# The down projection of a decoder block: accumulator loads and stores placed by step, second sums from copies, pools placed anew

## The chip, the cores and the metric

The kernel runs on one core of a Trainium2 chip. The metric is device time in microseconds (us) of one execution; the number for a kernel is the median of its runs. Engines are named as in the profile: PE is TensorE's matmuls, PEld its weight loads, DVE VectorE, ACT ScalarE, POOL GpSimd, SP the engine on whose queue this kernel issues its DMAs.

## The reference

One layer of a decoder: three token mixers side by side, an output projection, then a SwiGLU feed-forward block with its residual. All of it is float32. The change is in the last line, the down projection, the last stage of the kernel.

```python
D_MODEL = 1024; SEQ = 2048; D_FF = 2816
...
    x = x + mixed @ w_out[li]
    hn = rms_norm(x, norm_ffn_g[li])
    gate, up = jnp.split(hn @ w_ffn_up[li], 2, axis=-1)
    x = x + (jax.nn.silu(gate) * up) @ w_ffn_down[li]
return x
```

## The kernel before

A float32 matmul is done as three: each operand is split into a high part that the array takes exactly and the rest, and high x high, high x low and low x high are summed in PSUM. ACT makes the high part (L249, a copy that rounds), and VectorE or POOL the low part (L250, a difference).

The two feed-forward matmuls use a scheme of seven block products in place of eight (Winograd's form of Strassen's). In the **down stage** (L1492 on) the left operand is the gated activation (2048 x 2816), the right one the down weight (2816 x 1024), each cut into two by two blocks. The products are done in the order 1, 5, 6, 2, 3, 7, 4. A product has 11 steps of 128 rows of its inner dimension; each step is 24 matmuls, three for each of the eight PSUM banks (tile `dn`, bank i holds 128 rows by 512 columns of the product). All seven make 1848 matmuls.

For a step SP loads `ar` (left, 512 KB, L1514) and `br` (right, 256 KB, L1503). Products 5 and 7 load two right blocks and take their difference on POOL (L243); 5 keeps it in `xb`, and 6 and 4 go on from there. ACT then writes `dah` and `dbh`, VectorE `dal`, POOL `dbl`. `ar`, `dah`, `dal`, `dbh` and `dbl` have four buffers each, `br` five.

The result is summed in 16 accumulators `acc` of 128 x 1024 (512 KB each), which start as the residual (`x2_s` in DRAM, L1590). Accumulator i (0 to 7) holds the quarters c11 and c12, accumulator 8 + i holds c21 and c22. Behind each product `flush_dn` adds its eight banks to the quarters: product 1 to c11, and ACT keeps a copy `u`; 5 to c12 and c22; 6 to `u`, and `u` then to c21 on VectorE and to c12 and c22 on POOL; 2 to c11, 3 to c12, 7 to c21 and c22, 4 to c21. A half that is finished goes out by a DMA of 256 KB (`done`, L1551): c11 behind product 2, c12 behind 3, c22 behind 7, c21 behind 4.

The order of each engine's instructions is made by a scheduler from the order of the program, the data that each instruction needs and its own estimate of times; what `keep_in_program_order` wraps stays in the order of the program on its queue. An engine takes its instructions in order, and so does SP its DMAs: one that has to wait holds up those behind it. Places in SBUF come from pools; a pool opened at the left grows from low addresses, one at the right from high ones, and a tile placed where an older one lay waits for that one's last use.

Ahead of the down stage lies the **up stage**. For its last block of columns it does the seven products in the same order; its left operands `ah` and `al` of each product have a place of their own. The last product is 4. Behind it DVE and ACT finish the gated block `h` (DVE L1432 reads `c` for the last time), store it (`hs_s`, L1448) and make sums of it for the left operands of products 7, 5, 6 and 3 (`ls`, stored to `ls_s`, L1461).

Of the kernel before, what the change touches and what calls it, by code (L numbers as in the profile page):

```python
# [8 lines left out]
F32 = mybir.dt.float32  # L9
# [4 lines left out]
AF = mybir.ActivationFunctionType  # L14
# [5 lines left out]
P = 128  # L20
T = 2048
D = 1024
NT = T // P
# [39 lines left out]
def hybrid_block(ctx: ExitStack, tc: tile.TileContext, x, norm_mix_g, w_in, gla_w_decay,  # L63
                 gla_b_decay, gla_out_g, sb_q_g, sb_k_g, sb_out_g, hg_out_g, hg_lb_logits,
                 w_out, norm_ffn_g, w_ffn_up, w_ffn_down, out, dbg=None):
    nc = tc.nc
    x, out = x[0], out[0]
    w_in, w_out, w_up, w_dn = w_in[0], w_out[0], w_ffn_up[0], w_ffn_down[0]
    act, dve, pool, pe, dma = nc.scalar, nc.vector, nc.gpsimd, nc.tensor, nc.sync
# [54 lines left out]
    def open_pool(stack, name, bufs, space=None, side=None):  # L124
        kw = {} if space is None else {"space": space}
        if side is not None:
            kw["side"] = side
        return stack.enter_context(tc.tile_pool(name=name, bufs=bufs, reuse_waits="tile", **kw))
# [82 lines left out]
    def dt(name, shape, dtype=F32):  # L211
        return dram.tile(shape, dtype, name=name)
# [14 lines left out]
    x2_s = [dt(f"x2_s{t}", [P, D]) for t in range(NT)]  # L227
# [17 lines left out]
    def add(o, a, b, eng=dve):  # L245
        eng.tensor_tensor(o, a, b, op=ALU.add)  # L246
# [526 lines left out]
    with ExitStack() as ph:  # L773
        cn.open(ph)
        with ExitStack() as p1:
            stg = open_pool(p1, "s_g", 1)
            st = Stage(1, stg, open_pool(p1, "s_x", 2), True)
# [151 lines left out]
    with ExitStack() as ph:  # L929
# [28 lines left out]
        for g in G_ORDER:  # L958
            for h in range(0, SH, 2):
                for c in range(g, -1, -1):  # L960
                    for j in range(2):
                        u = Unit()
# [338 lines left out]

        folds = []
        done, total = 0.0, SH * sum(g + 0.625 for g in range(NG))
        step, wo_step = rec_steps(), load_wo()
        ns, n_slot = 0, 4 * len(units)
# [9 lines left out]
        for n in range(n_slot + LAG_A):  # L1315
            d = 0.0
            if n < n_slot:
                z_step(units[n // 4], n % 4)
                d = (n % 4 + 1) / 16 if units[n // 4].diag else 0.25
# [150 lines left out]
    for ip in range(2):  # L1470
        for n in range(NFF):
            f = n if ip == 0 else n // 2 + NK * (n % 2)
# [17 lines left out]


    pd = ExitStack()  # L1492
    bop = open_pool(pd, "g_bo", 4, side="right")
    lop = open_pool(pd, "g_lo", 4, side="right")
    accp = open_pool(pd, "g_acc", 1)
    rop = open_pool(pd, "g_ro", 1)
    psd = open_pool(pd, "g_psd", 8, PSUM)
    acc = []
# [6 lines left out]
    def left_dn(m, k):  # L1505
        nm = f"{m}_{k}"

        src = lop.tile([P, D], F32, tag="ar", name=f"ar{nm}")
        if m in (1, 2, 4):
            kh, j = {1: (0, 0), 2: (1, 0), 4: (1, 1)}[m]  # L1510
            at = hs_s[kh * NK + k][j].rearrange("p i j t -> p (i j t)")
        else:
            at = ls_s[m][k]
        tc.keep_in_program_order(dma.dma_start(src, at))  # L1514
        hi, lo = (lop.tile([P, D], F32R, tag=x, name=f"{x}{nm}") for x in ("dah", "dal"))
        conv_w(hi, lo, src, dve)
        return hi, lo

    def right_dn(m, k):
        nm = f"{m}_{k}"  # L1520

        def raw(kh, j):
            t_ = bop.tile([P, 512], F32, tag="br", name=f"br{nm}_{kh}{j}", bufs=5)
            load_b(t_, k, kh, j)
            return t_

        if m in (1, 2, 3):
            src = raw(*{1: (0, 0), 2: (1, 0), 3: (1, 1)}[m])
        elif m == 5:
            src = chain_b[k] = rop.tile([P, 512], F32, name=f"xb{k}")  # L1530
            load_b(src, k, 0, 1)
            sub(src, src, raw(0, 0), pool)
        elif m == 6:
            src = chain_b[k]
            sub(src, raw(1, 1), src, pool)
        elif m == 4:
            src = chain_b[k]
            sub(src, raw(1, 0), src, pool)
        else:
            src = raw(1, 1)  # L1540
            sub(src, src, raw(0, 1), pool)
        hi, lo = (bop.tile([P, 512], F32R, tag=x, name=f"{x}{nm}")
                  for x in ("dbh", "dbl"))
        conv_w(hi, lo, src)
        return hi, lo

    held, later = {}, []

    def done(t, hf):
        cs = slice(hf * 512, hf * 512 + 512)  # L1550
        dma.dma_start(out[t * P:(t + 1) * P, cs], acc[t][:, cs])  # L1551

    def flush_dn(m, i, ps):

        c11, c12 = acc[i][:, :512], acc[i][:, 512:]
        c21, c22 = acc[8 + i][:, :512], acc[8 + i][:, 512:]
        if m == 1:
            u = held[i] = rop.tile([P, 512], F32, name=f"u{i}")
            act.activation(u, ps, AF.Copy)
            add(c11, c11, ps)  # L1560
        elif m in (5, 7):
            c = {5: c12, 7: c21}[m]
            add(c, c, ps)
            add(c22, c22, ps)
            if m == 7:
                done(8 + i, 1)
        elif m == 6:
            u = held[i]
            add(u, u, ps)
            add(c21, c21, u)  # L1570
            later.append(lambda: add(c12, c12, u, pool))
            later.append(lambda: add(c22, c22, u, pool))
        else:
            c = {2: c11, 3: c12, 4: c21}[m]
            add(c, c, ps)
            done(*{2: (i, 0), 3: (i, 1), 4: (8 + i, 0)}[m])

    for m in (1, 5, 6, 2, 3, 7, 4):
        pss = [psd.tile([P, 512], F32, tag="dn", name=f"dn{m}_{i}") for i in range(8)]
        for k in range(NK):  # L1580
            (ah, al), (bh, bl) = left_dn(m, k), right_dn(m, k)
            for i in range(8):
                ts_ = slice(i * P, (i + 1) * P)
                pe.matmul(pss[i], ah[:, ts_], bh, start=(k == 0), stop=False)  # L1584
                pe.matmul(pss[i], ah[:, ts_], bl, start=False, stop=False)  # L1585
                pe.matmul(pss[i], al[:, ts_], bh, start=False, stop=(k == NK - 1))  # L1586
            if m == 1 and k == 2:
                for t in range(NT):
                    a = accp.tile([P, D], F32, name=f"acc{t}")
                    tc.keep_in_program_order(dma.dma_start(a, x2_s[t]))  # L1590
                    acc.append(a)
            for fn in later[:2]:
                fn()
            del later[:2]
        for i in range(8):
            flush_dn(m, i, pss[i])
    for fn in later:
        fn()
    pd.close()

    if dbg is not None:
# [29 lines left out]
```

## Time and profile before

| | us |
|---|---|
| median of 3 runs (lowest, highest) | 3063.36 (3062.43, 3068.29) |
| the profiled execution | 3067.76 |
| its span, first to last instruction | 3066.1 |
| last matmul of the up stage to last matmul of the down stage | 2578.05 to 3061.95 |
| PE busy in the whole span | 2796.4 (91%) |
| DVE, ACT, POOL busy in the whole span | 2052.4, 1320.5, 1463.2 |

The times are of one execution. PE's busy time counts pipelined matmuls with ends that are modelled, so a share of 91% says little of a single stage; one reads the stage by its own window and by what PE waited for. A wait is put down to the instruction that came last, and this one may itself have waited; the chain of waits goes further back. The granted clock is the share of full speed that TensorE got; it has two levels, 0.50 (1.2 GHz) and 1.00 (2.4 GHz), and a stretch may hold both.

### The profile page before, as it was taken

To read this page: it belongs to the slowest core of one execution; us is meant where nothing else is said; L and a number is where in the kernel's file an instruction comes from. 1 tells how busy PE (TensorE), PEld (TensorE's weight loads), DVE (VectorE), ACT (ScalarE), POOL (GpSimd) and SP (SyncE) were. 2 spreads that over 40 slices of the span, in tenths; PEclk is the share of its full clock that TensorE was granted. 3 is DMA by queue.
4 is the path that set the end of the run, shared out by engine and by line. 5 is a ranking of instruction groups with operands and counts; after the bars stand their busy time and mean duration, and the time that the engine had idled before them with its cause. 6 is when DMAs were issued, how large, how long until landed. Compare 5 with 4: busy or idle time off the path is not lost.

```text
span 3066.1 us, 45677 instructions
## 1 busy us (share of the span) xinstructions
PE 2796.4 (91%) x15906; PEld 2251.7 (73%) x15906; DVE 2052.4 (67%) x3621; ACT 1320.5 (43%) x2540; POOL 1463.2 (48%) x1412
## 2 busy tenths in 40 slices
PE   5898999998988999988878799999999998899988
PEld 4897778997656666655566588888788887787766
DVE  8887574987767787888877565556777775334233
ACT  5455444445666666765422333333433332322222
POOL 5341454343776666733221344444555553556244
PEclk7999999999788999999989899999999999999999
DMA  3543543343843333234354422222544445742354
GB/s 112 152 125 111 152 129 110 96 136 104 206 144 103 113 115 104 75 113 126 98 192 148 174 90 83 83 83 83 192 151 151 153 154 209 253 148 83 144 190 154
DMA packets 355206, 409.34 MB, mean 134 GB/s; under 512 B 59936, under 2 KB 262944, under 8 KB 353184
## 3 DMA queue, kind: packets, MB, share of 16 engines
q1 hardware_dynamic: 350880, 401.17, 41.1%
q0 software_dynamic: 4096, 5.25, 0.5%
q8 instruction: 127, 2.08, 0.3%
q14 instruction: 103, 0.84, 0.1%
HBM read 281.02 MB, written 125.30 MB: 133 GB/s over the span
## 4 chain that ended last, share of the span: by engine, by line
PE 59%; DVE 12%; DMA 5%; issue 4%; POOL 3%; ACT 2%; SPq 1%; DVEq 0%; POOLq 0%; ACTq 0%
PE gu L1420 9%; PE gu L1421 9%; PE gu L1419 9%; PE dn L1584 4%; PE dn L1585 4%; PE dn L1586 4%; PE z L104 3%; PE av L104 2%; DVE pr L1002 2%; PE wt L107 2%; DVE m L841 1%; PE sch L104 1%; DMA m<-mx_s 1%; PE scg L104 1%; PE ho L104 1%
## 5 line engine op out<-in xcount | busy, mean ns | idle before, releaser
L1420 PE MATMUL gu<-al,uh 128*128 128x512 f32 x1232 | 482.8, 392 | 7.7 <-DVE al L250 7.6
L1419 PE MATMUL gu<-ah,uh 128*128 128x512 f32 x1232 | 481.3, 391 | 4.8 <-ACT ah L249 4.8
L1421 PE MATMUL gu<-ah,ul 128*128 128x512 f32 x1232 | 481.1, 390 | 0.0
L250 POOL TENSOR_TENSOR ul<-bs,uh 128x512 fp32r<-128x512 f32 x176 | 247.7, 1408 | 224.4 <-ACT uh L249 224.4
L1009 POOL TENSOR_TENSOR w<-w,pr 128x512 f32<-128x512 f32 (+1 forms) x174 | 204.1, 1173 | 210.8 <-DVE pr L1002 109.0
L250 POOL TENSOR_TENSOR ul<-us,uh 128x512 fp32r<-128x512 f32 x132 | 186.1, 1411 | 215.5 <-ACT uh L249 185.9
L1584 PE MATMUL dn<-dbh,dah 128*128 128x512 f32 x616 | 238.7, 407 | 46.4 <-ACT dbh L249 46.4
L1420 PEld LDWEIGHTS gu<-al,uh 128*128 128x128 f32 x1232 | 232.2, 188 | 62.2 <-DVE al L250 14.4
L250 DVE TENSOR_TENSOR dal<-ar,dah 128x1024 fp32r<-128x1024 f32 x77 | 114.8, 1495 | 240.4 <-ACT dah L249 231.8
L1419 PEld LDWEIGHTS gu<-ah,uh 128*128 128x128 f32 x1232 | 232.5, 189 | 55.2 <-ACT ah L249 6.5
L1421 PEld LDWEIGHTS gu<-ah,ul 128*128 128x128 f32 x1232 | 232.3, 189 | 47.4
L1585 PE MATMUL dn<-dbl,dah 128*128 128x512 f32 x616 | 241.6, 392 | 4.0 <-POOL dbl L250 4.0
L249 ACT ACTIVATE uh<-bs 128x512 fp32r<-128x512 f32 x176 | 111.0, 632 | 308.0 <-PE gu L1420 284.4
L1586 PE MATMUL dn<-dbh,dal 128*128 128x512 f32 x616 | 240.6, 391 | 1.1 <-DVE dal L250 1.1
L249 ACT ACTIVATE dah<-ar 128x1024 fp32r<-128x1024 f32 x77 | 81.5, 1059 | 315.0 <-PE dn L1585 199.7
L246 DVE TENSOR_TENSOR h<-h,gu 128x512 f32<-128x512 f32 x176 | 120.4, 684 | 144.4 <-PE gu L1421 106.0
L104 PE MATMUL z<-sk,sq 128*128 128x512 f32 (+1 forms) x480 | 169.4, 437 | 14.1 <-ACT w L1001 8.6
L998 ACT ACTIVATE kp<-z 128x512 f32<-128x512 f32 (+1 forms) x240 | 127.8, 532 | 119.3 <-PE z L104 107.6
L1584 PEld LDWEIGHTS dn<-dbh,dah 128*128 128x128 f32 x616 | 120.7, 197 | 73.9 <-ACT dbh L249 48.5
L107 PE MATMUL wt<-ident,w 128*128 128x128 f32 x816 | 148.3, 296 | 14.1 <-POOL w L1009 12.1
L104 PEld LDWEIGHTS z<-sk,sq 128*128 128x128 f32 x480 | 79.6, 206 | 108.1 <-issue 44.4
L249 ACT ACTIVATE uh<-us 128x512 fp32r<-128x512 f32 x132 | 82.8, 630 | 166.8 <-PE gu L1420 90.6
(385 smaller groups left out, 7482.7 us busy)
## 6 DMA issues: line engine op xcount, KB each, us to landing
us<-in_w_ffn_up SPq DMA_DIRECT2D x88, 512.0 KB, 3.8
ls_s<-ls SPq DMA_DIRECT2D x44, 512.0 KB, 2.8
br<-in_w_ffn_down SPq DMA_DIRECT2D x88, 256.0 KB, 4.3
ar<-ls_s SPq DMA_DIRECT2D x44, 512.0 KB, 4.2
hs_s<-h SPq DMA_DIRECT2D x33, 512.0 KB, 2.6
ar<-hs_s SPq DMA_DIRECT2D x33, 512.0 KB, 4.4
sk<-sk_s SPq DMA_DIRECT2D x60, 256.0 KB, 3.1
st<-xs_s SPq DMA_DIRECT2D x14, 1024.0 KB, 5.2
```

Of the source, the lines that this page charges most:

```text
L104: self._add(nc.tensor.matmul(*a, **k))
L107: self._add(nc.tensor.transpose(*a, **k))
L249: act.activation(wh, st, AF.Copy)
L250: eng.tensor_tensor(wl, st, wh.bitcast(F32), op=ALU.subtract)
L998: act.activation(kp[:, :n], z, AF.Sigmoid, scale=-1.0)
L1009: pool.tensor_tensor(w, w, pr[:, 1:n + 1], op=ALU.mult)
L1419: pe.matmul(pv, bh[:, k, :], ah[:, :, k, :], start=(k == 0), stop=False)
L1420: pe.matmul(pv, bh[:, k, :], al[:, :, k, :], start=False, stop=False)
L1421: pe.matmul(pv, bl[:, k, :], ah[:, :, k, :], start=False, stop=(k == KH - 1))
L1584: pe.matmul(pss[i], ah[:, ts_], bh, start=(k == 0), stop=False)
L1585: pe.matmul(pss[i], ah[:, ts_], bl, start=False, stop=False)
L1586: pe.matmul(pss[i], al[:, ts_], bh, start=False, stop=(k == NK - 1))
```

## The change

Four things, all in the down stage:

- **Accumulator loads.** Before, all 16 are issued in one bundle behind the loads of step 2 of product 1. Now one is issued with each of the steps 2 to 9 of product 1 (accumulators 0 to 7) and of product 5 (8 to 15).
- **Stores.** Before, the eight stores of a finished quarter are issued where its sums are made, at the end of products 2, 3, 7 and 4. Now those of 2, 3 and 7 are put in a list, and each step but the first of the next product issues one, in program order. Those of product 4 stay at its end.
- **Second sums.** Behind products 5 and 7, ACT copies the bank to a tile `v`, VectorE adds the bank to the first quarter, and the sum with c22 is made later from `v` (before: VectorE added the bank twice). Behind 6 all three sums with `u` go into a list (before: c21 at once on VectorE, c12 and c22 in a list for POOL, two a step). The list is written out at one entry a step, on VectorE. Neither kind of sum is wrapped in `keep_in_program_order`.
- **Pools.** At the right, from the top down, now `acc`, then `lo` (`ar`, `dah`, `dal`), then `bo` (`br`, `dbh`, `dbl`); before `bo` and `lo` at the right, `acc` at the left.

Bytes of each partition, as the two programs place them:

| tiles | before | after | what lay there in the up stage (after) |
|---|---|---|---|
| `acc` | 19936 to 85472 | 163808 to 229344 | `ah`, `al` of products 2, 6, 5, 1 |
| `ar` | 153568 to 169952 | 114656 to 131040 | `ah`, `al` of product 4 (before: of 3, 2) |
| `dah`, `dal` | 169952 to 202720 | 131040 to 163808 | `ah`, `al` of products 7 and 3 |
| `br` | 202720 to 212960 | 88032 to 98272 | `c` in its first 3.5 KB, then nothing (before: of 5) |
| `dbh`, `dbl` | 212960 to 229344 | 98272 to 114656 | nothing |
| `u`, `xb`, and after `v` | 85472 to 124384 | 19936 to 75232 | right operands, sums `ls` |

```diff
--- before.py
+++ after.py
@@ -1490,9 +1490,9 @@
 
 
     pd = ExitStack()
+    accp = open_pool(pd, "g_acc", 1, side="right")
+    lop = open_pool(pd, "g_lo", 4, side="right")
     bop = open_pool(pd, "g_bo", 4, side="right")
-    lop = open_pool(pd, "g_lo", 4, side="right")
-    accp = open_pool(pd, "g_acc", 1)
     rop = open_pool(pd, "g_ro", 1)
     psd = open_pool(pd, "g_psd", 8, PSUM)
     acc = []
@@ -1544,36 +1544,43 @@
         conv_w(hi, lo, src)
         return hi, lo
 
-    held, later = {}, []
+    held, kept, later, stores = {}, {}, [], []
 
     def done(t, hf):
         cs = slice(hf * 512, hf * 512 + 512)
-        dma.dma_start(out[t * P:(t + 1) * P, cs], acc[t][:, cs])
+        tc.keep_in_program_order(dma.dma_start(out[t * P:(t + 1) * P, cs], acc[t][:, cs]))
+
+    def copy_of(d, x, i, ps):
+        t_ = d[i] = rop.tile([P, 512], F32, tag=f"{x}{i}", name=f"{x}{i}_{len(d)}")
+        act.activation(t_, ps, AF.Copy)
+        return t_
 
     def flush_dn(m, i, ps):
 
+
         c11, c12 = acc[i][:, :512], acc[i][:, 512:]
-        c21, c22 = acc[8 + i][:, :512], acc[8 + i][:, 512:]
+        if m > 1:
+            c21, c22 = acc[8 + i][:, :512], acc[8 + i][:, 512:]
         if m == 1:
-            u = held[i] = rop.tile([P, 512], F32, name=f"u{i}")
-            act.activation(u, ps, AF.Copy)
+            copy_of(held, "u", i, ps)
             add(c11, c11, ps)
         elif m in (5, 7):
             c = {5: c12, 7: c21}[m]
+            v = copy_of(kept, "v", i, ps)
             add(c, c, ps)
-            add(c22, c22, ps)
-            if m == 7:
-                done(8 + i, 1)
+            later.append((lambda: add(c22, c22, v), (8 + i, 1) if m == 7 else None))
         elif m == 6:
             u = held[i]
             add(u, u, ps)
-            add(c21, c21, u)
-            later.append(lambda: add(c12, c12, u, pool))
-            later.append(lambda: add(c22, c22, u, pool))
+            for j, c in enumerate((c12, c21, c22)):
+                sums[j].append((lambda c=c: add(c, c, u), None))
         else:
             c = {2: c11, 3: c12, 4: c21}[m]
             add(c, c, ps)
-            done(*{2: (i, 0), 3: (i, 1), 4: (8 + i, 0)}[m])
+            if m == 4:
+                done(8 + i, 0)
+            else:
+                stores.append((i, m - 2))
 
     for m in (1, 5, 6, 2, 3, 7, 4):
         pss = [psd.tile([P, 512], F32, tag="dn", name=f"dn{m}_{i}") for i in range(8)]
@@ -1584,18 +1591,23 @@
                 pe.matmul(pss[i], ah[:, ts_], bh, start=(k == 0), stop=False)
                 pe.matmul(pss[i], ah[:, ts_], bl, start=False, stop=False)
                 pe.matmul(pss[i], al[:, ts_], bh, start=False, stop=(k == NK - 1))
-            if m == 1 and k == 2:
-                for t in range(NT):
-                    a = accp.tile([P, D], F32, name=f"acc{t}")
-                    tc.keep_in_program_order(dma.dma_start(a, x2_s[t]))
-                    acc.append(a)
-            for fn in later[:2]:
+            if m in (1, 5) and k >= 2 and len(acc) < (8 if m == 1 else NT):
+                t = len(acc)
+                a = accp.tile([P, D], F32, name=f"acc{t}")
+                tc.keep_in_program_order(dma.dma_start(a, x2_s[t]))
+                acc.append(a)
+            if k and stores:
+                done(*stores.pop(0))
+            if later:
+                fn, st = later.pop(0)
                 fn()
-            del later[:2]
+                if st is not None:
+                    stores.append(st)
+        sums = [[], [], []]
         for i in range(8):
             flush_dn(m, i, pss[i])
-    for fn in later:
-        fn()
+        for l in sums:
+            later.extend(l)
     pd.close()
 
     if dbg is not None:
```

At the handover from the up stage, SP's queue. `hs_s` and `ls_s` as targets are stores of the last gated block and its sums. One piece of the difference:

```order
 L1514 DMA ar_0_25622<-hs_s_0_299 128x1024
+L1448 DMA hs_s_1_342<-h_21_25435 128x1024
+L1461 DMA ls_s_10_276<-ls_1_25582 128x1024
 L1503 DMA br_0_00_25628<-in_w_ffn_down 128x512
+L1461 DMA ls_s_10_287<-ls_0_25581 128x1024
 L1514 DMA ar_1_25658<-hs_s_0_301 128x1024
 L1503 DMA br_1_00_25664<-in_w_ffn_down 128x512
-L1448 DMA hs_s_1_342<-h_21_25435 128x1024
 L1514 DMA ar_2_25694<-hs_s_0_303 128x1024
-L1461 DMA ls_s_10_276<-ls_1_25582 128x1024
+L1461 DMA ls_s_10_265<-ls_0_25581 128x1024
 L1503 DMA br_2_00_25700<-in_w_ffn_down 128x512
```

The store of `h` and two stores of its sums now stand ahead of the first `br` or between the first loads, and the first `br` comes fourth.

At the end of product 2, SP's queue; `ar_0`, `br_0` are the loads of step 0 of product 3. Before:

```order
L1503 DMA br_10_10_27348<-in_w_ffn_down 128x512
L1551 DMA out<-acc_25730 128x512
L1551 DMA out<-acc_25732 128x512
L1551 DMA out<-acc_25734 128x512
L1551 DMA out<-acc_25736 128x512
L1551 DMA out<-acc_25738 128x512
L1551 DMA out<-acc_25740 128x512
L1551 DMA out<-acc_25742 128x512
L1551 DMA out<-acc_25744 128x512
L1514 DMA ar_0_27402<-ls_s_0_255 128x1024
L1503 DMA br_0_11_27408<-in_w_ffn_down 128x512
L1514 DMA ar_1_27438<-ls_s_1_256 128x1024
```

After:

```order
L1503 DMA br_10_10_27350<-in_w_ffn_down 128x512
L1514 DMA ar_0_27397<-ls_s_0_255 128x1024
L1503 DMA br_0_11_27403<-in_w_ffn_down 128x512
L1514 DMA ar_1_27434<-ls_s_1_256 128x1024
L1503 DMA br_1_11_27440<-in_w_ffn_down 128x512
L1551 DMA out<-acc_25730 128x512
L1514 DMA ar_2_27472<-ls_s_2_257 128x1024
L1503 DMA br_2_11_27478<-in_w_ffn_down 128x512
L1551 DMA out<-acc_25768 128x512
```

The eight stores stood ahead of all loads of product 3; now the first stands behind the loads of two steps, and each further one behind those of one more.

At the end of product 6, VectorE's queue; `u` are the copies of product 1 with product 6 added, `dal_3` and `dal_4` belong to steps 3 and 4 of product 2. Before:

```order
L246 TENSOR_TENSOR acc_25752<-acc_25752,u_26059 128x512
L246 TENSOR_TENSOR u_26071<-u_26071,dn_7_26534 128x512
L250 TENSOR_TENSOR dal_3_27083<-ar_3_27080,dah_3_27082 128x1024
L246 TENSOR_TENSOR acc_25754<-acc_25754,u_26062 128x512
L246 TENSOR_TENSOR acc_25756<-acc_25756,u_26065 128x512
L246 TENSOR_TENSOR acc_25758<-acc_25758,u_26068 128x512
L246 TENSOR_TENSOR acc_25760<-acc_25760,u_26071 128x512
L250 TENSOR_TENSOR dal_4_27121<-ar_4_27118,dah_4_27120 128x1024
```

After:

```order
L246 TENSOR_TENSOR u_7_26055<-u_7_26055,dn_7_26542 128x512
L246 TENSOR_TENSOR acc_25806<-acc_25806,u_2_26040 128x512
L246 TENSOR_TENSOR acc_26265<-acc_26265,u_2_26040 128x512 x2
L250 TENSOR_TENSOR dal_3_27088<-ar_3_27085,dah_3_27087 128x1024
L246 TENSOR_TENSOR acc_25844<-acc_25844,u_3_26043 128x512
L246 TENSOR_TENSOR acc_26306<-acc_26306,u_3_26043 128x512 x2
L246 TENSOR_TENSOR acc_25882<-acc_25882,u_4_26046 128x512
L246 TENSOR_TENSOR acc_26347<-acc_26347,u_4_26046 128x512 x2
...
L246 TENSOR_TENSOR acc_26470<-acc_26470,u_7_26055 128x512
L250 TENSOR_TENSOR dal_4_27125<-ar_4_27122,dah_4_27124 128x1024
```

Sums with `u` for c12 and c22, which POOL made before, now stand on VectorE, three for each `u`, and the scheduler has put them all ahead of the `dal` of step 4.

## Rows read from the trace of the kernel before

**Rows 1.** Waits: who waited for what; us in total, times, longest; 2575 to 3067.

```profile
PE dn L1584 <- ACT dbh L249: 46.4, 5, 14.6
...
PE dn L1585 <- POOL dbl L250: 4.0, 2, 2.2
...
PE dn L1586 <- DVE dal L250: 1.1, 1, 1.1
```

**Rows 2.** TensorE's timeline: start, length in us, work, idle before it and its releaser.

```profile
2580.96 3.68 PE L1584 MATMUL dn<-dbh,dah 128*128 128x512 f32 x8 [2.91 <-ACT dbh L249]
...
2615.10 1.22 PE L1584 MATMUL dn<-dbh,dah 128*128 128x512 f32 x2 [14.58 <-ACT dbh L249]
...
2799.06 0.50 PE L1585 MATMUL dn<-dbl,dah 128*128 128x512 f32 x1 [2.25 <-POOL dbl L250]
...
2852.99 3.78 PE L1584 MATMUL dn<-dbh,dah 128*128 128x512 f32 x8 [6.70 <-ACT dbh L249]
...
2924.94 1.65 PE L1584 MATMUL dn<-dbh,dah 128*128 128x512 f32 x3 [9.68 <-ACT dbh L249]
...
2999.59 1.65 PE L1584 MATMUL dn<-dbh,dah 128*128 128x512 f32 x3 [12.49 <-ACT dbh L249]
```

**Rows 3.** Windows of TensorE: from:to, length, busy (matmuls), granted clock, DMA share, GB/s.

```profile
2578.05:3061.95 483.90, 432.53 (x1848) 0.95 0.48 172
...
2799.60:2803.00 3.40, 3.40 (x9) 0.50 0.62 231
...
2999.60:3004.40 4.80, 4.80 (x11) 0.50 1.01 398
2629.00:2796.00 167.00, 167.00 (x739) 1.00 0.45 154
2590.00:2615.00 25.00, 10.52 (x47) 0.80 1.02 402
2615.00:2657.00 42.00, 41.90 (x177) 0.96 0.71 257
```

**Rows 4.** The chain of waits from 2840 to 2860: start, length in us, what.

```profile
2841.57 5.46 DVE acc L246 x8
...
2847.05 0.33 SPq L1551
...
2847.47 3.79 DMA ar<-ls_s
...
2851.36 0.85 ACT dah L249
...
2852.32 0.62 ACT dbh L249
```

**Rows 5.** SP's timeline: three of its DMA issues.

```profile
2581.86 0.47 SPq L1503 DMA_DIRECT2D br<-in_w_ffn_down  x1
...
2587.45 14.81 SPq L1590 DMA_DIRECT2D acc<-x_s  x16
...
2842.29 5.09 SPq L1551 DMA_DIRECT2D out<-acc  x8
```

**Rows 6.** Timelines of VectorE and ACT at the handover.

```profile
2580.20 1.22 DVE L246 TENSOR_TENSOR ls<-h,h 128x1024 f32<-128x1024 f32 x1
...
2587.90 0.63 ACT L249 ACTIVATE dbh<-br 128x512 fp32r<-128x512 f32 x1 [0.87 <-DMA br<-in_w_ffn_down]
```

**Rows 7.** By tile (`acc`, `dal`, `dbl`): times, ns min/median/max, first and last start.

```profile
L246 DVE TENSOR_TENSOR acc<-acc,dn x64: 671/682/689, 2657.2 to 3062.0; 128x512 f32<-128x512 f32 x64
...
L246 POOL TENSOR_TENSOR acc<-acc,u x16: 1272/1742/2268, 2776.3 to 2806.2; 128x512 f32<-128x512 f32 x16
L246 DVE TENSOR_TENSOR acc<-acc,u x8: 676/1480/1785, 2777.9 to 2791.6; 128x512 f32<-128x512 f32 x8
...
L250 DVE TENSOR_TENSOR dal<-ar,dah x77: 1208/1226/2348, 2583.6 to 3041.1; 128x1024 fp32r<-128x1024 f32 x77
...
L250 POOL TENSOR_TENSOR dbl<-br,dbh x44: 1277/1804/2282, 2581.0 to 2966.8; 128x512 fp32r<-128x512 f32 x44
```

## The prediction

> **What bounds the kernel now.** I read the waits of the engines in the down stage first, then TensorE's timeline where it starts again, then the windows, then the chain of waits ahead of one such start, and last SP's own timeline.
>
> The down stage lies between the last matmul of the up stage at 2578.05 us and its own last one at 3061.95 us. TensorE is busy for 432.53 of these 483.90 us [rows 3], so it stands for 51.4 us. The waits say for what: 46.4 us in five waits for `dbh`, 4.0 us in two for `dbl`, 1.1 us in one for `dal` [rows 1]. The five are 2.91 us at the handover from the up stage, 14.58 us ahead of 2615.10, and 6.70, 9.68 and 12.49 us at the ends of products 2, 3 and 7 [rows 2].
>
> ACT is named as the releaser, but it had been waiting itself. The chain ahead of 2852.99 shows for what [rows 4]: eight sums of product 2 on VectorE (5.46 us), the issue of the last store on SP, 3.79 us until the load of `ar` had landed, 0.85 and 0.62 us for the two conversions, then the first matmul. SP's queue is in order, the eight stores stand ahead of the next product's first load [rows 5], and each store waits for its sum. The starts at 2924.94 and 2999.59 repeat this. Ahead of 2615.10 the 16 accumulator loads stand in the queue instead: their issue took 14.81 us [rows 5], and 402 GB/s moved meanwhile [rows 3].
>
> Each of these starts is also slow. In six stretches behind a wait the granted clock is 0.50 (1.2 GHz) while TensorE works; the shortest, 3.4 us, and the longest, 4.8 us, are in [rows 3]. At a mean of 4.0 us, half of it lost, they cost 12.0 us. From 2629 to 2796, across the end of product 5, TensorE never waits and the clock stays at 1.00 (2.4 GHz); 739 matmuls take 167.00 us, 0.226 us each. A step of 24 is then 5.42 us, a product 59.7 us, and all 1848 are 417.6 us. The stage loses 66.3 us in all: 51.4 idle, 12.0 to the clock, 2.9 in what is left around the starts.
>
> **The change, part by part.** *Accumulator loads.* One load of 0.52 MB goes with each of 16 steps, behind that step's own loads. A step then moves 1.31 MB in product 1 and 1.57 MB in product 5 (it loads two right operands), in 5.42 us: 242 and 290 GB/s. From 2615 to 2657 the trace moves 257 GB/s with TensorE busy for 41.90 of 42.00 us, and 402 GB/s just before [rows 3]. I take no cost, since 402 was reached on the same queue with the same kind of load; the other bound is 257 GB/s as the limit, which makes a step of product 5 6.1 us and costs 0.7 us eight times, 5.5 us. The 14.58 us go.
>
> *Handover.* The new layout costs something here. The first `ar` now lies where the up stage keeps the left operand of its last product, and the first `br` where `c` lies, which VectorE reads last. In SP's order the first `br` now stands behind two stores, the second of which waits for the sum at 2580.20, finished at 2581.42 [rows 6]. So it is issued where the third `br` was, at 2581.86 [rows 5]. That third one was converted at 2587.90, as soon as it had landed [rows 6]: 6.0 us with three transfers of 0.52 MB just ahead of it in SP's order. Now two are ahead; one less, at 402 GB/s, is 1.3 us, so 4.7 us. The bounds are 6.0 us and the 3.79 us of [rows 4]. With 0.65 us for conversion and hand-off TensorE starts at 2587.2 (2586.3 to 2588.5) in place of 2580.96: 9.2 us idle (8.3 to 10.5), and one stretch at the low clock, 2.1 us (1.7 to 2.4). The `dbl` of that step, 1.80 us [rows 7], is covered by eight matmuls at half clock, about 3.6 us. No gain is possible here, since nothing lets the first `br` go earlier than before.
>
> *Stores.* Of 32 stores 24 move into the next product's steps, each behind the loads of two steps. What queues behind a waiting store is `ar` and `br` of step 2 onwards. The first store waits for the sum of bank 0, whose last matmul lies 21 x 0.226 = 4.7 us ahead of the product's end; with 0.68 us for the sum [rows 7] the queue is free 4 us before the end. The load lands 3.8 to 6.0 us later and is converted in 1.5 us, so step 2 is ready 3.5 us behind the end at the latest, and TensorE comes to it after two steps, 10.8 us. Some 7 us of cover; the 6.70, 9.68 and 12.49 us go, and three slow stretches with them.
>
> *Second sums from copies.* Sixteen copies of 0.62 us (the 128x512 form in [rows 4]) go to ACT, beside the first sum on VectorE, so a PSUM bank is free no later than after the two sums in a row of before. At the end of product 5 TensorE did not wait before, so I take nothing either way.
>
> *Sums of `u`.* Sixteen sums leave POOL, 1.74 us each, 28 us ahead of the `dbl` that TensorE waited for 4.0 us in all [rows 1, 7]; this goes, with a slow stretch. VectorE takes them, and the order shows that they are not spread: all 24 sums with `u` stand ahead of the `dal` of step 4. From bank 0's end, 4.7 us before the end of product 6, VectorE does eight sums out of PSUM (0.68 us), 24 out of SBUF, and three `dal` (1.23 us) [rows 7]. At 0.68 us a sum this is 25.4 us. TensorE needs that `dal` behind four steps and eight matmuls, 4.7 + 21.7 + 1.8 = 28.2 us after the same start. So it is 2.8 us early. I allow 1 us, for collisions with POOL.
>
> Sum: 63.4 us of idle and slow clock go; 9.2 + 2.1 + 1.0 = 12.3 us come or stay; 51.1 us net. Of the 2.9 us around six starts up to 2.4 go with five of them, so 51 to 53.5; I take 52. The profiled execution, 3067.76 us with its span of 3066.1, would be 3015.8; it lies 4.4 us over the median of the runs, and from that median it is 3063.36 - 52 = 3011 us. Differences under 0.2%, 6 us, can't be told from none here.
>
> **The rivals.** *VectorE becomes late behind product 6.* Sums with an operand in PSUM took 671 to 689 ns, whatever POOL did; those with both in SBUF took 676 to 1785, median 1480, beside POOL's own sums of 1272 to 2268 [rows 7]. The change gives VectorE 40 sums of the second kind, where 8 were. The Trainium skill ("SBUF — State Buffer", section "Who interferes with whom") says that a VectorE instruction with two SBUF inputs and a GpSimd instruction that reads SBUF block one another for the whole instruction, which speaks against taking the second sums from copies. By that rule, the trace agrees: only the sums with two SBUF operands vary. At 1.72 us each the 24 take 41.3 us in place of 16.3, `dal` is 22 us late, and a slow stretch adds 2: 3035 us. For it: the row. Against: POOL has only one `dbl` a step left there, so about five of the 24 sums can meet one; at 1.1 us more for each, 5.5, the wait is 2.7 us.
>
> *Short waits stay at the ends.* Waits of 2.25 and 1.7 us between 2796 and 2812 were enough for one slow stretch [rows 2, 3]. If each of the six product ends keeps 2 us of wait and 1.7 us of slow clock, 22 us come back, 3033 us. Against it: the end of product 5 shows none.
>
> *The early part gains nothing.* If the loads now in between hold up steps 1 to 10 as much as the bundle did, the 10.8 us that the first stretch gains (18.5 + 3.7 before, 9.2 + 2.1 after) are lost: 3022 us. The 257 GB/s with a busy TensorE speaks against it.
>
> *Slower.* The stores could take away SP's lead. Then a step's load starts only after the sum ahead of it, and a step would be issue, landing and conversion, 0.8 + 3.8 + 1.5 = 6.1 us, without cover on top of 5.42. In 24 steps that is 146 us, so 3157 us. It is slower than before once less than 3.9 of the 6.1 us are covered in each, that is, once a store is released less than 3.9 us ahead of the step it feeds. By the count above it is released about 14 us ahead.
>
> **How the numbers follow.** Forecast, 3011 us with a range of its own of 3004 to 3019 (4.7 us of doubt in the median, 5.5 us of transfers, 2.7 us on VectorE): 0.80. VectorE late: 0.05. Short waits: 0.06. Early part gains nothing: 0.06. Slower: 0.03. The range that leaves out no more than 2 in 10 takes in the early part and reaches towards the two waits: 3003 to 3030. Faster by over 0.2%: 0.96, the first four less a little for a shortfall of several at once; within 0.2%: 0.01; slower: 0.03.
>
> **What would show it.** Right: one TensorE wait of 8 to 11 us at the handover and none above 3 us behind it; the down stage some 431 us long; one slow stretch; `out` stores one at a time between loads on SP; `acc` loads one per step. Wrong in a part: a wait for `dal` about 22 us behind the end of product 6 (VectorE), waits for `dbh` in products 1 or 5 (transfers), waits at the third step of products 3, 7 or 4 (SP's lead). The whole is wrong if the windows show the clock at 0.50 in more than two places behind the handover.

## The result, and the profile after

The changed kernel takes 3012.09 us (median of 4 runs, 3009.24 to 3014.35); the kernel before 3062.89 us (3059.03 to 3068.29). The ratio is 0.983 with a 95% interval of 0.9815 to 0.985. The profiled execution took 3013.06 us with a span of 3011.3.

The up stage's last matmul ends at 2575.83 us and the down stage's last one at 3006.56. The stage is 430.73 us long where it was 483.90 [rows 3], 53.2 us less. Windows of TensorE in the kernel after (from:to, length, busy and matmuls of PE, then of PEld, DVE, ACT, POOL, granted clock, DMA share, GB/s): the stage, the time in which the accumulators are loaded, and the first matmuls of the stage.

```profile
core 0: us, PE busy (x) PEld busy (x) DVE busy (x) ACT busy (x) POOL busy (x), PEclk, DMA share, GB/s
2575.83:3006.56 430.73, 421.56 (x1848) 348.30 (x1848) 176.03 (x177) 136.44 (x179) 208.06 (x121) 0.99 0.55 196
2594.00:2660.00 66.00, 66.00 (x293) 54.65 (x292) 22.11 (x22) 26.27 (x36) 34.43 (x23) 1.00 0.90 324
...
2584.00:2588.00 4.00, 4.00 (x10) 3.17 (x11) 0.00 (x0) 0.14 (x1) 1.15 (x1) 0.50 0.88 247
```

TensorE works for 421.56 us and stands for 9.17, where it worked for 432.53 and stood for 51.37. So 42.2 of the 53.2 us are waits that are gone, and 11.0 are busy time: some 9.8 of it are matmuls that no longer run at the low clock (24 us of work at 0.50 before, by the six stretches of 4.0 us; 4.5 us after, 2583.85 to 2588.31), the rest lies around the starts. The second row answers to the 257 GB/s of [rows 3]: TensorE never stops while 324 GB/s come in.

The waits of the whole stage, and where they end, answer to [rows 1, 2]: eight have become two. The first block gives us in total, times and longest.

```profile
PE dn L1591 <- ACT dbh L249: 8.0, 1, 8.0
PE dn L1592 <- POOL dbl L250: 1.1, 1, 1.1
```

```profile
2583.85 0.80 PE L1591 MATMUL dn<-dbh,dah 128*128 128x512 f32 x1 [8.02 <-ACT dbh L249]
...
2788.89 0.50 PE L1592 MATMUL dn<-dbl,dah 128*128 128x512 f32 x1 [1.15 <-POOL dbl L250]
```

The first is the handover. On SP's timeline of the kernel after, the first `br` stands behind the store of `h` and a store of its sums:

```profile
2577.97 0.32 SPq L1448 DMA_DIRECT2D hs_s<-h  x1
2579.23 0.32 SPq L1461 DMA_DIRECT2D ls_s<-ls  x1
2579.60 0.45 SPq L1503 DMA_DIRECT2D br<-in_w_ffn_down  x1
```

and ACT converts it as soon as it has landed, with TensorE starting 0.68 us behind:

```profile
2583.17 0.63 ACT L249 ACTIVATE dbh<-br 128x512 fp32r<-128x512 f32 x1 [2.93 <-DMA br<-in_w_ffn_down]
```

The second wait is new in kind. Behind product 6 VectorE makes its sums with `u` in a run, and one `dbl` on POOL lasts as long as that run. VectorE's and POOL's timelines, kernel after:

```profile
2775.19 9.11 DVE L246 TENSOR_TENSOR acc<-acc,u 128x512 f32<-128x512 f32 x15
2784.22 3.48 DVE L250 TENSOR_TENSOR dal<-ar,dah 128x1024 fp32r<-128x1024 f32 x3
```

```profile
2777.88 10.96 POOL L250 TENSOR_TENSOR dbl<-br,dbh 128x512 fp32r<-128x512 f32 x1 [9.10 <-ACT dbh L249]
```

The other `dbl` took 1.27 to 2.3 us. This one began 2.7 us into the run and ended at 2788.84, 1.14 us behind the last of VectorE's `dal`. Most of the sums themselves were not held up: by tile, VectorE's in the kernel after are (ns, lowest/median/highest)

```profile
L246 DVE TENSOR_TENSOR acc<-acc,u x24: 676/677/1776, 2763.4 to 2783.6; 128x512 f32<-128x512 f32 x24
L246 DVE TENSOR_TENSOR acc<-acc,v x16: 677/686/1519, 2703.1 to 2952.3; 128x512 f32<-128x512 f32 x16
```

with a median of 0.68 us where the eight of before had 1.48 [rows 7].

### The profile page after: what moved, and what is told of

It is laid out like the page before. It is cut to its first block, busy times and chain, and to the rows that moved or that the text cites. A ratio compares the mean times of both kernels' runs of the same rounds, so it can differ in the third digit from the quotient of the medians.

```text
span 3011.3 us, 45677 instructions
## 1 busy us (share of the span) xinstructions
PE 2779.2 (92%) x15906; PEld 2240.4 (74%) x15906; DVE 2053.4 (68%) x3637; ACT 1329.6 (44%) x2556; POOL 1445.5 (48%) x1396
## 4 chain that ended last, share of the span: by engine, by line
PE 60%; DVE 12%; DMA 5%; issue 5%; ACT 2%; POOL 2%; SPq 0%; DVEq 0%; POOLq 0%; ACTq 0%
PE gu L1420 9%; PE gu L1421 9%; PE gu L1419 9%; PE dn L1591 4%; PE dn L1592 4%; PE dn L1593 4%; PE z L104 3%; DVE pr L1002 2%; PE av L104 2%; PE wt L107 2%; DVE m L841 1%; PE sch L104 1%; PE ho L104 1%; DMA wos<-in_w_out 1%; PE scg L104 1%
## 5 line engine op out<-in xcount | busy, mean ns | idle before, releaser
L1420 PEld LDWEIGHTS gu<-al,uh 128*128 128x128 f32 x1232 | 232.6, 189 | 62.4 <-DVE al L250 14.3
L250 DVE TENSOR_TENSOR dal<-ar,dah 128x1024 fp32r<-128x1024 f32 x77 | 107.4, 1398 | 222.2 <-ACT dah L249 209.3
L1002 DVE TENSOR_TENSOR_SCAN pr<-kp,pr,one 128x513 f32<-128x513 f32 x105 | 133.4, 1271 | 22.5 <-ACT kp L998 22.3
```

Source lines behind the costliest of these rows:

```text
L250: eng.tensor_tensor(wl, st, wh.bitcast(F32), op=ALU.subtract)
L1002: dve.tensor_tensor_scan(pr[:, n::-1], kr, ones[0].to_broadcast([P, n + 1]) if ones else kr, u.carry[b], op0=ALU.mult, op1=ALU.bypass)
L1420: pe.matmul(pv, bh[:, k, :], al[:, :, k, :], start=False, stop=False)
```

## The experiments

In the profiled executions the up stage's end lies up to 10 us apart, and the whole time moves with it. The length of the down stage, from the up stage's last matmul to its own, leaves this out; but each length is that of one execution, and how far it scatters was not measured, so a difference of a few us is read together with the waits. All kernels in one table (us; the ratio, with its 95% interval, is to runs of the kernel before made along with that kernel, whose median lay between 3062.80 and 3064.21 for e1 to e11; none where there is a single run):

| kernel | stage | idle | PE busy | time | ratio |
|---|---|---|---|---|---|
| before | 483.90 | 51.37 | 432.53 | 3062.89 | |
| after | 430.73 | 9.17 | 421.56 | 3012.09 | 0.9832 (0.9815 to 0.9850) |
| e1: after, pools as before | 426.41 | 5.03 | 421.38 | 3006.22 | 0.9813 (0.9790 to 0.9837) |
| e2: after, loads bundled | 445.36 | 22.51 | 422.85 | 3026.37 | 0.9877 (0.9853 to 0.9901) |
| e3: after, stores at the ends | 468.73 | 39.98 | 428.75 | 3045.35 | 0.9944 (0.9921 to 0.9966) |
| e4: after, sums as before | 435.67 | 12.44 | 423.23 | 3017.40 | 0.9845 (0.9825 to 0.9864) |
| e5: before, stores spread | 449.77 | 21.72 | 428.05 | 3027.90 | |
| e6: before, loads spread | 469.87 | 38.73 | 431.14 | 3046.51 | |
| e7: after, sums in program order | 432.00 | 9.88 | 422.12 | 3013.15 | 0.9838 (0.9821 to 0.9854) |
| e8: e1 and e7 | 427.17 | 6.74 | 420.43 | 3005.99 | 0.9812 (0.9797 to 0.9827) |
| e9: after, stores one step earlier | 431.26 | 9.55 | 421.71 | 3011.86 | |
| e10: after, stores ahead of loads | 445.55 | 19.93 | 425.62 | 3025.14 | 0.9876 (0.9861 to 0.9890) |
| e11: e1, sums of `u` spread | 427.04 | 3.66 | 423.38 | 3004.94 | 0.9802 (0.9784 to 0.9821) |

**Each part undone.** e1 lays the pools out as before:

```diff
-    accp = open_pool(pd, "g_acc", 1, side="right")
-    lop = open_pool(pd, "g_lo", 4, side="right")
     bop = open_pool(pd, "g_bo", 4, side="right")
+    lop = open_pool(pd, "g_lo", 4, side="right")
+    accp = open_pool(pd, "g_acc", 1)
```

> The changed kernel with its three pools laid out as in the kernel before; loads, sums and stores stay as changed. On the SP engine the first right-hand tile's load then stands second again, ahead of the loads of the up stage's other left blocks. Theory (the layout costs at the handover and the spread loads do not need it): the wait of TensorE for its first dbh falls from 8.02 us to about 2.9 us, as in the kernel before [rows 2], every later product stays free of waits, and the time is some 5 us below that of the changed kernel (3012), so about 3007, ratio to the kernel before about 0.982. Rival (the accumulator tiles need the places that the new layout gives them, or the first spread loads wait for the up stage's last readers): the handover wait falls but waits of 5 us or more for ar or br appear in the first product, and the time is 3012 or above.

The waits of e1's stage:

```profile
PE dn L1591 <- ACT dbh L249: 2.9, 1, 2.9
PE dn L1592 <- POOL dbl L250: 1.1, 1, 1.1
PE dn L1593 <- DVE dal L250: 1.1, 1, 1.1
```

The handover wait is back at 2.9 us and no other has come but 1.1 us for a `dal`, which the kernel before had too [rows 1]. The new layout costs 4.3 us of stage, and the spread loads do not need it.

e2 bundles the accumulator loads again:

```diff
-            if m in (1, 5) and k >= 2 and len(acc) < (8 if m == 1 else NT):
-                t = len(acc)
-                a = accp.tile([P, D], F32, name=f"acc{t}")
-                tc.keep_in_program_order(dma.dma_start(a, x2_s[t]))
-                acc.append(a)
+            if m == 1 and k == 2:
+                for t in range(NT):
...
```

> The changed kernel with the 16 accumulator loads put back as one bundle behind the third step of the first product; layout, sums and stores stay as changed. Theory (a bundle uses up SP's lead, the spread hides the loads whole): one wait of 10 to 15 us comes back in the first product (14.58 us in the kernel before [rows 2]) with a stretch at half clock behind it that costs 2 to 2.5 us, so 3024 to 3029, ratio about 0.988. Rival (the gain in the early part came from the layout, not from the spread): no wait above 3 us there and a time within 3 us of 3012.

One wait of 13.16 us came back behind the handover's 8.21:

```profile
PE dn L1591 <- ACT dbh L249: 21.4, 2, 13.2
PE dn L1592 <- POOL dbl L250: 1.1, 1, 1.1
```

The stage is 14.6 us longer, the time 14.3 us. So the spread, not the layout, took this wait away.

e3 puts the stores back at the ends of products 2, 3 and 7:

```diff
-                stores.append((i, m - 2))
+                done(i, m - 2)
...
-            later.append((lambda: add(c22, c22, v), (8 + i, 1) if m == 7 else None))
+            if m == 7:
+                add(c22, c22, v)
+                done(8 + i, 1)
+            else:
+                later.append((lambda: add(c22, c22, v), None))
```

> The changed kernel with the output stores back at the ends of the products 2, 3 and 7, eight in a row each; loads, layout and copies stay as changed (the second sum of product 7 is made at its end, so that its store can stand there). Theory (eight stores in a row in front of the loads of the next product cost SP's lead): three waits of some 6.7, 9.7 and 12.5 us, as in the kernel before [rows 2], 28.9 us in sum, and three stretches at half clock of 2 to 2.5 us each: 3045 to 3048, ratio about 0.995. Rival (these waits came from the double sums that held PSUM and VectorE, not from the stores): at most 5 us above 3012.

The waits at the three ends are 7.12, 10.34 and 13.25 us; the stage is 38.0 us longer, of which 30.8 are idle and 7.2 busy time, in the main slow clock:

```profile
PE dn L1595 <- ACT dbh L249: 38.8, 4, 13.2
PE dn L1596 <- POOL dbl L250: 1.1, 1, 1.1
```

Behind products 2 and 3 neither kernel makes double sums, and behind 7 this one takes only the first from PSUM; but both still stand at its end there. What speaks against the rival is e5 below, which keeps the double sums from PSUM and has no wait at these ends.

e4 takes the second sums as before, from PSUM in products 5 and 7, and splits the sums of `u` between VectorE and POOL:

```diff
-            v = copy_of(kept, "v", i, ps)
...
-            later.append((lambda: add(c22, c22, v), (8 + i, 1) if m == 7 else None))
+            add(c22, c22, ps)
...
-            for j, c in enumerate((c12, c21, c22)):
-                sums[j].append((lambda c=c: add(c, c, u), None))
+            add(c21, c21, u)
+            later.append(lambda: add(c12, c12, u, pool))
+            later.append(lambda: add(c22, c22, u, pool))
```

> The changed kernel with the second sums as before: straight from PSUM in products 5 and 7, and the u sums split between VectorE (one) and POOL (two a step); loads, stores and layout stay as changed. Theory (sums on POOL delay its dbl): waits of about 4.0 us for dbl come back in the product after product 6 with a stretch at half clock of 1.5 to 2 us, the single wait of 1.15 us goes, so 4 to 5 us above the changed kernel, about 3016 to 3017. Rival (moving the u sums to VectorE only moved the same collision, since one dbl took 10.96 us there beside a run of fifteen sums): within 1.5 us of 3012 either way.

Two waits for `dbl`, 2.31 and 1.70 us, are back and the one of 1.15 is gone; the stage is 4.9 us longer, of which 3.3 are idle (0.4 of them at the handover). The medians lie 5.3 us apart with intervals that overlap.

```profile
PE dn L1593 <- ACT dbh L249: 8.4, 1, 8.4
PE dn L1594 <- POOL dbl L250: 4.0, 2, 2.3
```

e4 undoes the copies `v` and the move of the `u` sums together, so what each is worth alone stays open.

Undone one at a time, the parts cost 14.6 + 38.0 + 4.9 - 4.3 = 53.2 us of stage, as much as all of them together. So near a match is partly luck, since what the low clock costs at the handover alone differs by 2 us and more between kernels (last section).

**Two parts alone, on the kernel before.** e5 has the list of stores and nothing else, e6 the loads one to a step and nothing else; their edits are those of the change.

> The kernel before with nothing changed but the stores of products 2, 3 and 7, which go one to a step of the following product. Theory (the parts add up: taking the spread stores out of the changed kernel made the down stage 38.0 us longer, 430.73 to 468.73): the stage falls by 36 to 40 us, 483.90 to 444 to 448, with the waits of 6.70, 9.68 and 12.49 us gone and the one of 14.58 us left. Rival (the stores can be spread only once the double PSUM sums of products 5 and 7 are gone): waits of 3 us or more stay at the starts of products 3, 7 or 4.

> The kernel before with nothing changed but the 16 accumulator loads, one to a step from the third step on; layout, sums and stores as before. Theory (bundling them again in the changed kernel cost 14.6 us of stage, 430.73 to 445.36, and the old layout does not hinder them): the wait of 14.58 us goes with its slow stretch, and the stage falls by 14 to 17 us, to 467 to 470, with the handover wait still at 2.9 us. Rival (in the old layout the loads wait for places of the up stage): waits above 3 us for ar or br stay in the first product.

e5 shortens the stage by 34.1 us, less than the 36 expected at the least. Its three waits at the ends are gone, 28.9 us, and of five waits for `dbh` the two of the handover and of product 1 are left:

```profile
PE dn L1587 <- ACT dbh L249: 17.0, 2, 14.1
```

What is short of 36 us is the clock at the handover: behind its wait there the first 8 us of e5 ran at 0.50, those of the kernel before at 0.79 (last section). e6 shortens the stage by 14.0; the long wait of product 1 is gone, those at the ends stand at 6.85, 9.78 and 12.43 us. The waits for `dbl` grew from 4.0 to 5.6 us, and why is not shown:

```profile
PE dn L1585 <- ACT dbh L249: 32.0, 4, 12.4
PE dn L1586 <- POOL dbl L250: 5.6, 2, 3.3
```

Both parts work without the others.

**How much lead the stores need.** In products 3 and 7, e9 lets the first store stand behind the loads of one step, e10 ahead of any. In product 4 the stores wait for sums that its own steps make, so there e9 changes nothing and e10 leaves the loads of one step ahead of the first:

```diff
-            if k and stores:
+            if stores:
                 done(*stores.pop(0))
```

```diff
+            if stores:
+                done(*stores.pop(0))
             (ah, al), (bh, bl) = left_dn(m, k), right_dn(m, k)
...
-            if k and stores:
-                done(*stores.pop(0))
```

> The changed kernel with each store one step earlier: the first store of a product stands behind the loads of one step of the next, not of two. In the changed kernel the load behind the first store of product 2 was converted at 2829.7 and TensorE came to that step some 8.3 us later (2827.1 + 10.9). Theory (the cover is a matter of steps of lead): one step less leaves 2.8 us of cover, so no wait at the starts of products 3 and 7 and a down stage within 1 us of 430.73. Rival (the stores hold SP up in each step, so that less lead shows in every one): waits of several us within products 3 and 7 and a stage longer by 10 us or more.

> The changed kernel with each store ahead of the loads of its step, and with the first step of a product included: the first store stands behind no load of the next product. Theory: the cover is gone (8.3 - 10.9 = -2.6 us), so a wait of 1.7 to 2.6 us at the starts of products 3 and 7 with a slow stretch of 1 to 2 us lost behind each, the steps behind it undisturbed: 5 to 9 us in all, 3017 to 3021, stage 436 to 440. Rival 1 (the stores then hold up every step): 20 us or more. Rival 2 (the lead does not matter, only that the stores are single): no wait, 3012.

e9 has one new wait of 0.36 us, at the start of product 7, and its stage is 0.5 us longer. e10 has 2.69 us at the start of product 3, near the count, but 6.14 at that of product 7 and 1.47 early in product 4; its stage is 14.8 us longer, more than the 5 to 9 expected. TensorE's timeline of e10:

```profile
2823.51 0.50 PE L1593 MATMUL dn<-dbh,dah 128*128 128x512 f32 x1 [2.69 <-ACT dbh L249]
...
2891.41 0.80 PE L1593 MATMUL dn<-dbh,dah 128*128 128x512 f32 x1 [6.14 <-ACT dbh L249]
...
2959.08 0.50 PE L1593 MATMUL dn<-dbh,dah 128*128 128x512 f32 x1 [1.47 <-ACT dbh L249]
```

Why product 7 needs more stands in the kernel after, on ACT's timeline, at the step behind the first store of products 3 and 7:

```profile
2828.11 1.06 ACT L249 ACTIVATE dah<-ar 128x1024 fp32r<-128x1024 f32 x1 [10.56 <-DMA ar<-ls_s]
2829.08 0.62 ACT L249 ACTIVATE dbh<-br 128x512 fp32r<-128x512 f32 x1
...
2888.36 1.06 ACT L249 ACTIVATE dah<-ar 128x1024 fp32r<-128x1024 f32 x1 [10.97 <-DMA ar<-ls_s]
2892.49 0.63 ACT L249 ACTIVATE dbh<-br 128x512 fp32r<-128x512 f32 x1 [3.07 <-POOL br L243]
```

In product 3 `dbh` follows `dah` at once. In product 7 it waits for POOL's difference of two right blocks and comes 4.1 us behind. VectorE's first sum behind product 2 starts at 2822.32, 21 matmuls of 0.227 us ahead of its end, so product 3 starts at 2827.1; TensorE needs the step at 2838.0 and the operand is ready at 2829.7, 8.3 us early. Product 7 starts 59.8 us later and needs its own at 2897.8, with the operand ready at 2893.1, 4.7 us early. With two steps of lead (10.9 us) less, 8.3 becomes a wait of 2.6 and 4.7 one of 6.2: the 2.69 and 6.14 of e10. With one step less, 4.7 becomes a wait of 0.7, and e9 shows 0.36.

**The long `dbl`.** e7 keeps `dal` and the sums from the list in the order of the program on VectorE, so that they alternate:

```diff
-        conv_w(hi, lo, src, dve)
+        act.activation(hi, src, AF.Copy)
+        tc.keep_in_program_order(dve.tensor_tensor(lo, src, hi.bitcast(F32), op=ALU.subtract))
...
-                fn()
+                tc.keep_in_program_order(fn())
```

> The changed kernel with the sums of u and v held on VectorE in the order of the program, one between the dal of two steps, so that the run of fifteen sums in 9.11 us behind product 6 is gone; all else as changed. Theory (a run of VectorE sums with both inputs in SBUF kept POOL out: one dbl took 10.96 us beside it, where the others took 1.29 to 1.8): the longest dbl of the down stage falls to 2.5 us or less, the wait of 1.15 us for dbl goes, and the down stage is 429 to 430 us long in place of 430.73; in the time of runs that can't be told from none. Rival (the long dbl comes from something else, such as its two SBUF inputs landing late): a dbl of 5 us or more stays and so does the wait.

By tile, POOL's `dbl` from `br` and VectorE's sums of `u` in e7:

```profile
L250 POOL TENSOR_TENSOR dbl<-br,dbh x44: 1281/1745/2268, 2575.9 to 2922.4; 128x512 fp32r<-128x512 f32 x44
```

```profile
L246 DVE TENSOR_TENSOR acc<-acc,u x24: 677/1775/1782, 2761.7 to 2883.1; 128x512 f32<-128x512 f32 x24
```

The long `dbl` is gone, and so is the wait; now 14 of the 24 sums take 1.78 us instead, and each of them began while an instruction of POOL was under way: VectorE waits for POOL. The stage did not get shorter, though, which I had expected: `dal` of a product's first step, which the scheduler had put among the sums out of PSUM, now stands behind all eight of them, and two waits of 0.78 us for it came in, in products 5 and 6.

```profile
PE dn L1592 <- ACT dbh L249: 8.3, 2, 8.0
PE dn L1594 <- DVE dal L1517: 1.6, 2, 0.8
```

**Put together.** e8 is e1 and e7 in one. e11 is e1 with only the sums of `u`, and the `dal` of steps 3 on of products 2 and 3, kept in order.

> Both together: pools laid out as in the kernel before, and the sums of u and v held in the order of the program. Theory (the two parts do not touch each other): the down stage takes the 426.41 us of the run with the old layout, less 1 to 1.5, so about 425 us, and the time is about 3005, ratio to the kernel before about 0.981, some 6 us below the changed kernel. Rival (with the earlier handover the spread loads and the sums held in order meet, dal comes late): waits for dal above 2 us and a down stage of 428 us or more.

> The run with the old layout, and in it only the sums of u (products 2 and 3) held in program order between the dal of two steps; the dal of a product's first three steps and the sums of v are left free, since holding them all put waits of 0.78 us for dal at the starts of two products. Theory: no long dbl, so the wait of 1.07 us for dbl goes and no wait for dal comes at the starts of products; the down stage is some 425.3 us (426.41 - 1.07) and the time about 3005, ratio to the kernel before 0.981. Rival (sums and dal in one row delay dal in products 2 and 3): waits for dal of 0.5 us or more there and a stage of 427 us or more.

e8 has the handover wait of e1, the two of 0.78 us of e7, and one for `dal` of 2.20 us behind the handover, where e1 has 1.06; its stage is 427.17 us, no better than e1's 426.41. e11 has only 3.66 us of waits left, as meant,

```profile
PE dn L1594 <- ACT dbh L249: 2.9, 1, 2.9
PE dn L1596 <- DVE dal L1517: 0.8, 1, 0.8
```

but its stage is 427.04 us, since more of it ran at the low clock (busy 423.38 us where e1 has 421.38). The three with the old layout take 3005 to 3006 us and can't be told apart. They lie 6 to 7 us below the changed kernel; their intervals overlap with its own, and what speaks for the gain is the stage, 3.6 to 4.3 us shorter, with the handover wait at 2.9 in place of 8.0 us in each of the three.

## Why the prediction was right, point by point

The forecast of 3011 us and a stage of some 431 us came out at 3012.09 and 430.73. It held by its own steps but for the landing at the handover and for who paid behind product 6, and e1 to e4 show the four parts at nearly the sizes they were given. That it came within 1 us is partly luck, since four runs of the changed kernel lie over 5 us.

- **Accumulator loads:** priced at nothing, with 5.5 us as the other bound. 324 GB/s beside a TensorE that never stopped shows that 257 GB/s was no limit; e2 and e6 show that the spread is what removes the wait.
- **Handover:** predicted 9.2 us (8.3 to 10.5), measured 8.02, under that range. Its parts: the first `br` is issued 3.77 us behind the up stage's end (predicted 3.81), lands and is converted from 3.57 us later (predicted 4.7, bounds 3.79 and 6.0), and TensorE starts 0.68 us behind (0.65). The mis-sized term is the landing, which lay below the lower bound: the step that failed was to take an `ar` of 512 KB [rows 4] as the floor for a `br` of 256 KB; whether it is the size that made it land sooner was not tried. The slow stretch behind it is there (4.00 us at 0.50 in the window above).
- **Stores:** three waits and three slow stretches went, as said, and the rival of a lost lead did not come. The cover of 7 us was one number for all products; it is 8.3 us in product 3 and 4.7 in product 7. The count took one right block a step and left out the second one and POOL's difference. It decided nothing at two steps of lead; at none (e10) it is 3.5 of the 5.8 us by which the stage went over what I expected there.
- **Sums of `u`:** 4.0 us of waits for `dbl` went, as predicted, and 1.0 us was allowed for collisions between VectorE and POOL, where one wait of 1.15 came. The size was right and the payer was not: I had VectorE's sums getting longer, and its `dal` late, as the rival at 3035 us. It was POOL that was held, and VectorE's sums got shorter. The Trainium skill ("SBUF — State Buffer", section "Who interferes with whom") leaves that open, since by it the order of issue decides which of the two blocks. By that, the trace agrees on who waits: in the changed kernel VectorE's run had begun 2.7 us ahead of the `dbl` of 10.96 us, and in e7 a `dbl` began at 2761.35, ahead of the sum at 2761.66 that took 1.78 us. On how long it differs: that section speaks of one instruction, the 10.96 us here are those of a whole run, and the measurement decides.
- **Copies `v`:** priced at nothing either way. No TensorE wait stands at the ends of products 5 and 7; e4 doesn't part them from the sums of `u`.
- **Idle and clock:** 51.4 - 10.2 = 41.2 us of waits were to go and 42.2 went; 9.9 us of slow clock and up to 2.4 around the starts were to go, and 11.0 went in all.

Of the rivals, the short waits at the ends and the lost early part did not come: no wait stands at the end of any product, and none in products 1 and 5.

The stage gained 53.2 us and the medians 50.8. The profile of before lay 4.9 us over its median and the profile of after 1.0 us over its own, which the prediction had met by taking its 52 us from the median.

## What to carry to other kernels

When a queue in order carries loads, and stores that wait for sums, count for each store how many steps of loads stand ahead of it; 24 stores of 256 KB, spread one to a step behind two steps of loads, brought no wait here, nor did 16 loads of 512 KB spread one to a step; in bundles they cost 38.0 and 14.6 us. Make that count for the product whose operands take longest to get ready, not for the usual one. When places in SBUF are laid out anew, look first at what the very first load then stands behind on its queue: here it took back 4.3 of 57.5 us.

## What the runs showed of the hardware that was not expected

A run of fifteen VectorE sums with both operands in SBUF and three `dal` held one POOL instruction of the same kind for 10.96 us, where it takes 1.27 to 2.3 otherwise; it came to its end 1.14 us behind the run. With sums and `dal` alternating (e7) it was VectorE that waited, 1.78 us a sum in place of 0.68, and no `dbl` took over 2.28. VectorE was busy back to back in e7 too (2760.5 to 2771.5), so why POOL got in there and not in the run is not shown. The long `dbl`, 10.88 to 10.96 us, is in all six kernels with the new sums in which the scheduler was free to place them (after, e1, e2, e3, e9, e10), and in no other.

The same wait can leave the clock in different states. At the handover TensorE stood for 2.91 us in e8, e1 and e11, and its first 8 us behind it had these granted clocks (windows of e8, e1 and e11, columns as above):

```profile
2576.40:2584.40 8.00, 5.80 (x24) 4.45 (x25) 7.93 (x6) 3.02 (x4) 4.19 (x3) 1.00 1.02 351
```

```profile
2576.50:2584.50 8.00, 6.94 (x22) 5.20 (x23) 7.97 (x6) 3.08 (x4) 4.11 (x3) 0.79 1.02 348
```

```profile
2572.50:2580.50 8.00, 7.25 (x16) 5.20 (x17) 7.96 (x6) 3.01 (x4) 4.19 (x3) 0.50 1.02 347
```

1.00, 0.79 and 0.50. Within these 8 us the three also waited for a `dal`, for 2.20, 1.06 and 0.76 us, so they are not quite alike, and it was the one with the longest such wait that kept its clock. The kernel before and e5, whose edit lies far behind the handover, part in the same way after waits of 2.91 and 2.90 us there (windows of before and e5):

```profile
2581.00:2589.00 8.00, 6.95 (x22) 5.21 (x23) 7.96 (x6) 3.07 (x4) 4.17 (x3) 0.79 1.01 351
```

```profile
2575.20:2583.20 8.00, 7.25 (x16) 5.24 (x17) 7.97 (x6) 3.03 (x4) 4.35 (x3) 0.50 0.99 348
```

At 0.79 the low clock costs 1.7 us of the 8, at 0.50 up to 4: as much as a part of the change like the sums brings. What makes the difference was not tried. The clock is enough to account for the 1.9 us by which e5 fell short of what I expected of it.
